# Up projection of a mixture-of-experts layer: the bias added over a whole PSUM bank by VectorE, the bounds applied by GpSimd

## The chip, the cores and the metric

The kernel runs on one core of a Trainium2 chip. The metric is device time in microseconds, the median of several executions. Its engines are TensorE (PE in the profile, PEld for its weight loads), VectorE (DVE), ScalarE (ACT), GpSimd (POOL) and SyncE (SP), which issues most DMAs. Each engine works through its own instructions in program order and waits on semaphores for the others.

## The reference, cut to what matters

The model is one layer on 1024 tokens of width 1024: a token mixer, then a channel mixer with 32 experts, of which every token uses four. The change lies in the channel mixer alone. For each expert and the token slots routed to it (`xb`):

```
up = xb @ w_up[e] + b_up[e]                     # 1024 -> 2048
x_glu, x_lin = split(up, 2)                     # gate half, linear half
x_glu = minimum(x_glu, 7)
x_lin = clip(x_lin, -7, 7)
act = x_glu * sigmoid(1.702 * x_glu) * (x_lin + 1)
y = act @ w_down[e] + b_down[e]                 # 1024 -> 1024
```

The rows `y` are weighted by the router's gates and added to the token's sum; a final norm ends the program. Everything is float32.

## The kernel before

**Where the time lies.** Up to about 590 us the kernel does the token mixer and the routing. The expert stage follows, and after it the last norm.

**Experts.** Expert r (in order of load) gets a fixed number of slots, `CAPS[r]`, from 210 down to 108. They run in the order `ORDER`, a small one and a large one in turn: 112, 210, 114, 192, 116, 182, 120, 174, 122, 168, 122, 164, 124, 160, 126, 158, 128, 154, 128, 150, 130, 148, 132, 146, 134, 142, 136, 140, 136, 138, 108, 108 slots. Twenty have more than 128. The last one (`tail`) is treated apart.

**Phases.** For an expert j the kernel has three phases: A computes the gate half of the up projection ("G"), B the linear half ("L"), D the down projection. Experts overlap: A(j), D(j-1), B(j), A(j+1), D(j), B(j+1) and so on. A phase has eight slots, one for each block k of 128 contracted rows; in slot k TensorE multiplies eight output blocks (m), each with three products of f16 parts (high by high, high by low, low by high; L1787 to L1789). The moving operand has as many columns as the expert has slots, n. The five experts above 170 slots or marked `tail` have phases of four output blocks instead.

**Weights.** SP loads one 128x1024 float32 piece for each slot into one of 14 staging buffers (`wf`, L1766). ScalarE makes its high f16 part (`wh`, L1886) and VectorE its low part (`wl`, L1887, which reads `wf` and `wh` from SBUF). The two are split six slots ahead of TensorE (`LOOK`), into seven buffers.

**PSUM.** A phase accumulates in a tile `ac` of three banks of 512 float32, two tiles taking turns. A bank holds `per = 512 // n` blocks: four up to 128 slots, three up to 170, two above.

**Epilogues.** The epilogue of a phase runs during the next phase: `run_phases` calls each of its pieces at a given slot, before that slot's matmuls, and after it the split for six slots on. Halves of four blocks (or two) are treated one after the other.

- Epilogue of A, during D: at slots 0 and 1 `clamp` writes `eg` from PSUM, one VectorE operation for each block, which adds the bias (one value per partition) and applies the upper bound (L1804). At slots 1 and 3 `gate` has ScalarE compute the sigmoid (`es`, L1809) and GpSimd multiply `eg` by it (L1810).
- Epilogue of B, during the next A: at slots 0 and 1 `lin` writes `el` in the same way (L1826); at slots 1 and 2 `prod` applies the lower bound and multiplies by `eg` (L1830); at slots 2 and 3 ScalarE writes the high part of the activation `aT` (`high`, L1837) and VectorE its low part (`low`, L1840). `aT` feeds the next D.
- Epilogue of D, during B: ScalarE moves the output to SBUF (`yT`, L1858) at slots 0 and 1; from slot 3 on TensorE turns it into rows (L1872), ScalarE scales them (`yr`, L1873), and GpSimd adds them to the sum in HBM by an indirect DMA (`acc_d`, L1875): at slot 4 for the first 128 rows, at slot 6 for the rest, where there is one.

**GpSimd's other work.** At slot 5 of each A it loads the slot list of a later expert (`ids`, L1720) and gathers the rows of the one after next (`xr`, L1730). All of this stands in GpSimd's one queue in program order. The rows are turned at the first slots of A (L1742, L1743).

Of the kernel before, what the change touches and what calls it, by code (L numbers as in the profile page):

```python
# [35 lines left out]
STRIDE = 1152  # L36
# [5 lines left out]
CAPS = [210, 192, 182, 174, 168, 164, 160, 158, 154, 150, 148, 146, 142, 140, 138, 136,  # L42
        136, 134, 132, 130, 128, 128, 126, 124, 122, 122, 120, 116, 114, 112, 108, 108]
# [80 lines left out]
def build(ctx, tc, A, out, dbg=None):  # L124
    nc = tc.nc
    V, S, G, PE, SY = nc.vector, nc.scalar, nc.gpsimd, nc.tensor, nc.sync
    dbg = dbg or {}
    MULT, ADD, SUB, MIN, MAX = OP.mult, OP.add, OP.subtract, OP.min, OP.max
# [6 lines left out]
    def pst(shape=(128, 512), dt=F32, tag="g"):  # L135
        return ps.tile(list(shape), dt, name=f"ps_{tag}", bufs=BANKS[tag])
# [117 lines left out]
    for r0, src in ((0, A["b_mod"]), (48, A["c"]), (56, A["norm1_w"]), (64, A["norm2_w"])):  # L254
        n = src.shape[1] // 128
# [62 lines left out]
    p = pst(tag="o")  # L318
# [77 lines left out]
    f = math.factorial  # L396
# [813 lines left out]
    for l in range(SL):  # L1210
        r = SL - 1 - l
# [16 lines left out]
    for i in range(-1, NT):  # L1228
        h = i + 1
        n = 2 if left["s5"] else 1  # L1230
# [317 lines left out]
    for i in range(NT):  # L1548
        h, b, t = i + 1, i - 1, i - 2
        hd, ob, ot, last = h < NT, 0 <= b, 0 <= t, i == NT - 1  # L1550
        f = lambda: fill(w3)
# [37 lines left out]
    t, b, i = NT - 3, NT - 2, NT - 1  # L1589
# [41 lines left out]
    SS = SW * SX  # L1631
    SA = 16.0
    with tc.manual_schedule():
# [6 lines left out]
        p = tpt()  # L1640
# [15 lines left out]
        p = tpt()  # L1656
# [14 lines left out]
        BALL = mc.tile([128, NE, 24], F32, name="BALL")  # L1671
# [26 lines left out]

    class Expert:
        def __init__(self, n, e, row, bias, q, tail=False):  # L1700
            self.n, self.get_e, self.get_row, self.bias, self.q = n, e, row, bias, q
            self.eid = None
            self.rows = [(0, min(n, 128))] + ([(128, n - 128)] if n > 128 else [])
            self.per = 512 // n
            every, lo, hi = list(range(8)), [0, 1, 2, 3], [4, 5, 6, 7]
            fits = 3 * self.per >= 8
            self.down = [every] if fits else [lo, hi]
            if fits and not tail:
                self.up = [[("G", every)], [("L", every)]]
            else:  # L1710
                self.up = [[("G", lo), ("L", lo)], [("G", hi), ("L", hi)]]
            self.xT = self.aT = self.yT = self.glu = self.final = None
# [39 lines left out]
    class Phase:  # L1752
# [41 lines left out]
        def halves(self):  # L1794
            return [(i, self.ms[i:i + self.nm // 2]) for i in range(0, self.nm, self.nm // 2)]

        def glu_pieces(self):
            x, n = self.x, self.x.n

            def clamp(i, ms):  # L1800
                if i == 0:
                    x.glu = mx.tile([128, self.nm, n], F32, name="eg", bufs=1)
                for q, m in enumerate(ms):
                    V.tensor_scalar(x.glu[:, i + q, :], self.loc(i + q), x.bias(m), 7.0 * SS, op0=ADD, op1=MIN)  # L1804

            def gate(i, ms):
                g = x.glu[:, i:i + len(ms)].rearrange("p m n -> p (m n)")
                s = mx.tile([128, len(ms) * n], F32, name="es", bufs=1)
                S.activation(s, g, AF.Sigmoid, scale=1.702 / SS)  # L1809
                G.tensor_tensor(g, g, s, op=MULT)  # L1810

            out = []
            for q, (i, ms) in enumerate(self.halves()):
                out += [(q, lambda i=i, ms=ms: clamp(i, ms)), (1 + 2 * q, lambda i=i, ms=ms: gate(i, ms))]
            return sorted(out, key=lambda t: t[0])

        def lin_pieces(self):
            x, n = self.x, self.x.n
            if x.aT is None:
                x.aT = mx.tile([128, 2, 8, n], F16, name="aT")  # L1820
            t = {}

            def lin(i, ms):
                t[i] = mx.tile([128, len(ms), n], F32, name="el")
                for q, m in enumerate(ms):
                    V.tensor_scalar(t[i][:, q, :], self.loc(i + q), x.bias(8 + m), 8.0 * SS, op0=ADD, op1=MIN)  # L1826
                t[i] = t[i].rearrange("p m n -> p (m n)")

            def prod(i, ms):
                V.scalar_tensor_tensor(t[i], t[i], -6.0 * SS, x.glu[:, i:i + len(ms)].rearrange("p m n -> p (m n)"),  # L1830
                                       op0=MAX, op1=MULT)

            def part(q, ms):
                return x.aT[:, q, ms[0]:ms[0] + len(ms), :].rearrange("p m n -> p (m n)")

            def high(i, ms):
                S.activation(part(0, ms), t[i], AF.Copy, scale=SA / (SS * SS))  # L1837

            def low(i, ms):
                V.scalar_tensor_tensor(part(1, ms), t[i], SA / (SS * SS), part(0, ms), op0=MULT, op1=SUB)  # L1840

            out = []
            for q, (i, ms) in enumerate(self.halves()):
                for at, f in ((0, lin), (1, prod), (2, high), (2, low)):
                    out.append((q + at, lambda i=i, ms=ms, f=f: f(i, ms)))
            return sorted(out, key=lambda t: t[0])

# [81 lines left out]
    def make(r):  # L1929
        def load(eng):  # L1930
            return eng.value_load(ordi[0:1, r:r + 1], min_val=0, max_val=NE - 1)

        return Expert(CAPS[r], lambda: load(SY), lambda q: load(q) * STRIDE, lambda m: BALL[:, r, m:m + 1], G,
                      r == ORDER[-1])

    class FinalNorm:
# [3 lines left out]
        def load(self, i):  # L1940
            x = self.x[i] = stg.tile([128, D], F32, name="wf")
            SY.dma_start(x, acc_d[i * 128:(i + 1) * 128, :])
# [91 lines left out]
    with tc.If(over > 0):  # L2034
        G.indirect_dma_start(out=acc_d[:, :], out_offset=bass.IndirectOffsetOnAxis(ap=ex[-1].ids[0][:, 0:1], axis=0),
                             in_=last.y, in_offset=None)
        bias_d = dram.tile([NE, 128, 24], F32, name="bias_d")
        for r in range(NE):
            SY.dma_start(bias_d[r], BALL[:, r, :])
        val = mc.tile([1, 4, 256], F32, name="oval")  # L2040
        v8 = [val[:, q, :].rearrange("p (r j) -> p r j", j=8) for q in range(4)]
        V.tensor_tensor_scan(val[:, 0, :], ones[0:1, 0:1].to_broadcast([1, 256]),
                             nbf.rearrange("p r j -> p (r j)"), 0.0, op0=MULT, op1=ADD)
        V.tensor_tensor(val[:, 0, :], val[:, 0, :], nbf.rearrange("p r j -> p (r j)"), op=MULT)
        V.tensor_copy(v8[1], ordf[:, 0:NE, None].to_broadcast([1, NE, 8]))
        V.scalar_tensor_tensor(v8[2], v8[1], float(STRIDE), cc("thr", 1).rearrange("p (r j) -> p r j", j=8),
                               op0=MULT, op1=ADD)
        V.tensor_copy(v8[3], cc("iota", 1)[:, 0:NE, None].to_broadcast([1, NE, 8]))
        vb = mc.tile([64, 4, 256], F32, name="ovb")
        for q in range(4):  # L2050
            p = tpt()
            PE.matmul(p[0:64, 0:256], ones[0:1, 0:64], val[:, q, :], start=True, stop=True)
            V.tensor_copy(vb[:, q, :], p[0:64, 0:256])
        V.tensor_scalar(vb[:, 0, :], vb[:, 0, :], -1.0, cc("pcol", 64), op0=ADD, op1=OP.is_equal)
        oc = mc.tile([64, 3], F32, name="ocol")
        ol = mc.tile([1, 3, 64], I32, name="olist")
        p = tpt()
        for q in range(3):
            V.tensor_tensor(vb[:, q + 1, :], vb[:, q + 1, :], vb[:, 0, :], op=MULT)
            V.tensor_reduce(oc[:, q:q + 1], vb[:, q + 1, :], op=ADD, axis=AX.X)  # L2060
            PE.transpose(p[0:1, q * 64:(q + 1) * 64], oc[:, q:q + 1], ident[0:64, 0:64])
        V.tensor_copy(ol.rearrange("p q s -> p (q s)"), p[0:1, 0:192])
        with tc.For_i(0, over, 1) as bi:
            e = SY.value_load(ol[0:1, 0, ds(bi, 1)], min_val=0, max_val=NE - 1)
            row = SY.value_load(ol[0:1, 1, ds(bi, 1)], min_val=0, max_val=(NE - 1) * STRIDE + T)
            ri = SY.value_load(ol[0:1, 2, ds(bi, 1)], min_val=0, max_val=NE - 1)
            bt = mx.tile([128, 24], F32, name="bt", bufs=1)
            SY.dma_start(bt, bias_d[ds(ri, 1)].rearrange("o p m -> (o p) m"))
            x = Expert(128, lambda: e, lambda q: row, lambda m: bt[:, m:m + 1], SY, True)
            x.load_ids()  # L2070
            x.gather()
            for _, t in x.turn_x():
                t()
            run_phases(x.phases("A") + x.phases("B") + x.phases("D"), {}, 3, 2)
            fin = FinalNorm()
            for i in range(NT):
                fin.load(i)
                fin.square(i)
                fin.store(i)
# [27 lines left out]
```

## Time and profile before

| | us |
|---|---|
| median of 3 executions | 1909.22 (1908.97 to 1916.93) |
| profiled execution, its own time | 1911.87 |
| span of its trace | 1910.2 |

| engine | busy us | share of the span |
|---|---|---|
| PE | 1753.9 | 92% |
| DVE | 1583.3 | 83% |
| ACT | 1236.3 | 65% |
| POOL | 575.1 | 30% |

The share of busy time is a mean over stages with different limits, so a stage is read by itself: its busy times, its waits, and the chain of work that ended last. A row of a timeline gives the start and the length of one instruction, or of several of one kind in a row (`x4`); in square brackets stands how long the engine stood idle before it, and what it then waited for. A wait is put down to whatever came last by the profile; where the engine named had long been done, it was another, often a DMA.

### The profile page before, as it was taken

The page shows a single profiled execution, that of the slowest core. Times are in us where ns is not written, and L with a number is a line of the kernel's source. Part 1 is how long each engine was busy: PE and PEld are TensorE (multiplying, and loading weights), DVE is VectorE, ACT ScalarE, POOL GpSimd, SP SyncE. Part 2 cuts the span into 40 slices and gives each one's busy share as a digit, 9 for nine tenths or more (in the row PEclk, how much of TensorE's full clock was granted, in tenths as well). Part 3 has the DMA queues.
Part 4 walks back from the last instruction along what each step waited for, and adds up shares of the span by engine and source line. Part 5 has one row for each costly group of instructions (what it writes and reads, how often), then busy time and mean ns, then how long its engine had stood idle before and what let it go on. Part 6 is the DMA issues. An engine that isn't in the chain of part 4 may idle for free.

```text
span 1910.2 us, 57330 instructions
## 1 busy us (share of the span) xinstructions
PE 1753.9 (92%) x23174; PEld 1559.7 (82%) x23174; DVE 1583.3 (83%) x2430; ACT 1236.3 (65%) x1714; POOL 575.1 (30%) x505
## 2 busy tenths in 40 slices
PE   6889988999974999999999989999999999999983
PEld 3756665556643899999999979999999999999973
DVE  7858677765576888888897969999999999999985
ACT  2722333212234777777787868888888888888874
POOL 3834110143434223132221413213133333233214
PEclk9989999999996999999999989999999999999997
DMA  8841246632229999999998989999999999999996
GB/s 293 285 103 39 59 148 201 215 128 71 72 81 287 335 317 288 355 327 336 329 346 285 365 268 380 368 367 372 361 371 355 366 365 341 369 374 354 364 327 206
DMA packets 189451, 533.54 MB, mean 279 GB/s; under 512 B 37710, under 2 KB 47880, under 8 KB 189148
## 3 DMA queue, kind: packets, MB, share of 16 engines
q1 hardware_dynamic: 167548, 490.92, 71.6%
q0 software_dynamic: 21344, 37.85, 8.3%
q8 instruction: 183, 3.00, 0.6%
q10 hardware_dynamic: 288, 1.05, 0.1%
q14 instruction: 88, 0.72, 0.1%
HBM read 489.81 MB, written 39.30 MB: 277 GB/s over the span
## 4 chain that ended last, share of the span: by engine, by line
PE 46%; DMA 12%; ACT 4%; DVE 3%; issue 3%; POOL 1%; SPq 0%; DVEq 0%; ACTq 0%; POOLq 0%
PE ac L1787 14%; PE ac L1788 14%; PE ac L1789 14%; DMA wf<-in_w_up_dram 10%; ACT wh L1886 3%; DVE wl L1887 2%; PE tp L1872 2%; PE tp L1742 2%; DMA wf<-in_w_down_dram 2%; DMA xr<-h2s,ids 1%; ACT yT L1858 1%; POOL fs L1948 0%; ACT yr L1873 0%; DMA idtab<-pairs,dest 0%; POOL fs L1949 0%
## 5 line engine op out<-in xcount | busy, mean ns | idle before, releaser
L1887 DVE SCALAR_TENSOR_TENSOR wl<-wf,wh 128x1024 f16<-128x1024 f32 x768 | 944.5, 1270 | 137.3 <-ACT wh L1886 127.5
L1886 ACT ACTIVATE wh<-wf 128x1024 f16<-128x1024 f32 x768 | 774.3, 1055 | 50.3 <-DMA wf<-in_w_up_dram 21.4
L1789 PE MATMUL ac<-xT,wl 128*128 128x122 f16 (+27 forms) x4096 | 770.3, 226 | 4.5 <-DVE wl L1887 4.5
L1787 PE MATMUL ac<-xT,wh 128*128 128x122 f16 (+27 forms) x4096 | 770.9, 226 | 3.2 <-DVE el L1826 1.4
L1788 PE MATMUL ac<-xT,wh 128*128 128x122 f16 (+27 forms) x4096 | 770.4, 226 | 0.6 <-ACT xT L1743 0.6
L1789 PEld LDWEIGHTS <-wl 128*128 128x128 f16 x6144 | 602.2, 98 | 10.9 <-DVE wl L1887 8.8
L1788 PEld LDWEIGHTS <-wh 128*128 128x128 f16 x6144 | 603.4, 98 | 5.5 <-issue 4.1
L1787 PEld LDWEIGHTS <-wh 128*128 128x128 f16 x6144 | 602.9, 98 | 5.5 <-ACT wh L1886 3.6
L1787 PE MATMUL ac<-aT,wh 128*128 128x122 f16 (+27 forms) x2048 | 380.0, 226 | 3.1 <-DVE eg L1804 2.0
L1789 PE MATMUL ac<-aT,wl 128*128 128x122 f16 (+27 forms) x2048 | 380.0, 225 | 1.8 <-DVE wl L1887 1.7
L1788 PE MATMUL ac<-aT,wh 128*128 128x122 f16 (+27 forms) x2048 | 380.0, 225 | 0.9 <-DVE aT L1840 0.9
L1875 POOL DMA_INDIRECT acc_d<-yr,ids x51 | 135.2, 2651 | 592.2 <-ACT yr L1873 409.0
L1810 POOL TENSOR_TENSOR eg<-eg,es 128x420 f32<-128x420 f32 (+28 forms) x74 | 102.5, 1385 | 301.7 <-ACT es L1809 301.7
L1858 ACT ACTIVATE yT<-ac,BALL,g2s 128x122 f32<-128x122 f32 (+27 forms) x256 | 97.7, 473 | 9.1 <-PE ac L1789 9.1
L1837 ACT ACTIVATE aT<-el 128x420 f16<-128x420 f32 (+28 forms) x74 | 45.2, 611 | 90.2 <-DVE el L1830 89.3
L1743 ACT COPY xT<-tp 128x1024 f16<-128x1024 f16 (+27 forms) x104 | 75.8, 730 | 29.9 <-PE tp L1742 29.5
L1730 POOL DMA_INDIRECT xr<-h2s,ids x52 | 85.7, 1647 | 30.8 <-issue 19.7
L1809 ACT ACTIVATE es<-eg 128x420 f32<-128x420 f32 (+28 forms) x74 | 44.8, 605 | 74.3 <-DVE eg L1804 72.2
L1742 PE MATMUL tp<-id,xr 128*128 128x128 f16 (+27 forms) x832 | 54.3, 204 | 29.6 <-DMA wf<-in_w_up_dram 22.8
L1872 PE MATMUL tp<-C,yT 128*128 128x128 f32 (+27 forms) x408 | 68.4, 281 | 13.4 <-ACT yT L1858 10.1
L1826 DVE TENSOR_SCALAR el<-ac,BALL 128x122 f32<-128x122 f32 (+27 forms) x256 | 75.9, 355 | 0.0
L1804 DVE TENSOR_SCALAR eg<-ac,BALL 128x122 f32<-128x122 f32 (+27 forms) x256 | 74.8, 355 | 0.0
(495 smaller groups left out, 2426.0 us busy)
## 6 DMA issues: line engine op xcount, KB each, us to landing
wf<-in_w_up_dram SPq DMA_DIRECT2D x512, 512.0 KB, 8.4
wf<-in_w_down_dram SPq DMA_DIRECT2D x256, 512.0 KB, 10.0
wst<-in_w_mod_dram SPq DMA_DIRECT2D x40, 512.0 KB, 4.4
wst<-in_w_in_dram SPq DMA_DIRECT2D x16, 576.0 KB, 5.5
x<-in_x_dram SPq DMA_DIRECT2D x16, 512.0 KB, 4.4
hTb<-hT_d SPq DMA_DIRECT2D x16, 512.0 KB, 5.4
wA<-in_w_mod_dram SPq DMA_DIRECT2D x8, 512.0 KB, 10.3
hT_d<-hTa SPq DMA_DIRECT2D x8, 512.0 KB, 5.5
```

The lines of the kernel that those rows point to most:

```text
L1730: G.indirect_dma_start(out=x, out_offset=None, in_=h2s[:, :], in_offset=bass.IndirectOffsetOnAxis(ap=self.ids[j][:, 0:1], axis=0))
L1742: PE.transpose(p[:, k, :], self.xr[j][:, kk_ * 128:(kk_ + 1) * 128], id16[0:c, 0:c])
L1787: PE.matmul(dst, h[:, ms], xh, start=k == 0 and m % x.per == 0, stop=False, skip_group_check=True)
L1788: PE.matmul(dst, h[:, ms], xl, start=False, stop=False, skip_group_check=True)
L1789: PE.matmul(dst, l[:, ms], xh, start=False, stop=k == 7, skip_group_check=True)
L1810: G.tensor_tensor(g, g, s, op=MULT)
L1826: V.tensor_scalar(t[i][:, q, :], self.loc(i + q), x.bias(8 + m), 8.0 * SS, op0=ADD, op1=MIN)
L1858: S.activation(x.yT[:, m, :], self.loc(i), AF.Identity, scale=g2s[:, m:m + 1], bias=x.bias(16 + m))
L1872: PE.transpose(p[0:c, m * 128:(m + 1) * 128], x.yT[:, q * 4 + m, r0:r0 + c], ident)
L1875: G.indirect_dma_start(out=acc_d[:, :], out_offset=bass.IndirectOffsetOnAxis(ap=x.ids[j][:, 0:1], axis=0), in_=y, in_offset=None, compute_ ...
L1886: S.activation(h, w, AF.Copy, scale=SW)
L1887: V.scalar_tensor_tensor(l, w, SW, h, op0=MULT, op1=SUB)
```

## The change

For all experts but the last, the bias and the bounds come apart. VectorE adds the biases of all blocks of a half that lie in one PSUM bank in a single TENSOR_TENSOR, with the bias broadcast over the slots. GpSimd then applies the bounds in place in SBUF, one TENSOR_SCALAR for each half: the upper bound for `eg`, both for `el`. `prod` on VectorE is left with a plain product. The sigmoid and the product of the gate come one slot later, and so do `prod`, `high` and `low`.

```diff
+        def add_bias(self, dst, i, count, b0):
+            x, n = self.x, self.x.n
+            a = i
+            while a < i + count:
+                k = min(i + count, (a // x.per + 1) * x.per) - a
+                o = (a % x.per) * n
+                V.tensor_tensor(dst[:, a - i:a - i + k, :],
+                                self.ac[:, a // x.per, o:o + k * n].rearrange("p (m n) -> p m n", m=k),
+                                x.bias(b0 + self.ms[a], k)[:, :, None].to_broadcast([128, k, n]), op=ADD)
+                a += k
...
             def clamp(i, ms):
                 if i == 0:
                     x.glu = mx.tile([128, self.nm, n], F32, name="eg", bufs=1)
+                if not x.tail:
+                    g = x.glu[:, i:i + len(ms)]
+                    self.add_bias(g, i, len(ms), 0)
+                    g = g.rearrange("p m n -> p (m n)")
+                    G.tensor_scalar(g, g, 7.0 * SS, None, op0=MIN)
+                    return
                 for q, m in enumerate(ms):
                     V.tensor_scalar(x.glu[:, i + q, :], self.loc(i + q), x.bias(m), 7.0 * SS, op0=ADD, op1=MIN)
...
-            out = []
+            out, late = [], int(not x.tail)
             for q, (i, ms) in enumerate(self.halves()):
-                out += [(q, lambda i=i, ms=ms: clamp(i, ms)), (1 + 2 * q, lambda i=i, ms=ms: gate(i, ms))]
+                out += [(q, lambda i=i, ms=ms: clamp(i, ms)), (1 + 2 * q + late, lambda i=i, ms=ms: gate(i, ms))]
...
             def lin(i, ms):
                 t[i] = mx.tile([128, len(ms), n], F32, name="el")
-                for q, m in enumerate(ms):
-                    V.tensor_scalar(t[i][:, q, :], self.loc(i + q), x.bias(8 + m), 8.0 * SS, op0=ADD, op1=MIN)
+                if x.tail:
+                    for q, m in enumerate(ms):
+                        V.tensor_scalar(t[i][:, q, :], self.loc(i + q), x.bias(8 + m), 8.0 * SS, op0=ADD, op1=MIN)
+                else:
+                    self.add_bias(t[i], i, len(ms), 8)
                 t[i] = t[i].rearrange("p m n -> p (m n)")
+                if not x.tail:
+                    G.tensor_scalar(t[i], t[i], 8.0 * SS, -6.0 * SS, op0=MIN, op1=MAX)

             def prod(i, ms):
-                V.scalar_tensor_tensor(t[i], t[i], -6.0 * SS, x.glu[:, i:i + len(ms)].rearrange("p m n -> p (m n)"),
-                                       op0=MAX, op1=MULT)
+                g = x.glu[:, i:i + len(ms)].rearrange("p m n -> p (m n)")
+                if x.tail:
+                    V.scalar_tensor_tensor(t[i], t[i], -6.0 * SS, g, op0=MAX, op1=MULT)
+                else:
+                    V.tensor_tensor(t[i], t[i], g, op=MULT)
...
+            late = int(not x.tail)
             for q, (i, ms) in enumerate(self.halves()):
-                for at, f in ((0, lin), (1, prod), (2, high), (2, low)):
+                for at, f in ((0, lin), (1 + late, prod), (2 + late, high), (2 + late, low)):
                     out.append((q + at, lambda i=i, ms=ms, f=f: f(i, ms)))
```

The rest of the diff hands `tail` to the expert and lets `bias` return several blocks' values.

## Rows read from the trace of the kernel before

**Rows 1.** The page, part 4: the chain that ended last, its shares by engine.

```profile
PE 46%; DMA 12%; ACT 4%; DVE 3%; issue 3%; POOL 1%; SPq 0%; DVEq 0%; ACTq 0%; POOLq 0%
```

**Rows 2.** The same chain in order of time, its longest pieces: start us, us, what.

```profile
1097.81 30.94 DMA wf<-in_w_up_dram
...
1141.24 0.61 PE tp L1872 x4
...
1803.09 0.67 DVE aT L1840
```

**Rows 3.** Busy us by stretch: PE, PEld, DVE, ACT, POOL; then clock, DMA share, GB/s.

```profile
700.00:1141.00 441.00, 425.36 (x6353) 416.25 (x6350) 373.21 (x462) 340.95 (x451) 108.86 (x72) 0.98 0.95 322
1141.00:1803.00 662.00, 661.76 (x10777) 655.98 (x10778) 628.09 (x768) 566.83 (x749) 205.25 (x124) 1.00 1.01 365
...
1682.58:1758.56 75.98, 75.98 (x1253) 75.09 (x1251) 72.21 (x89) 65.66 (x89) 24.58 (x13) 1.00 1.00 360
```

**Rows 4.** All waits of PE from 1141 to 1803 us: total us, times, longest.

```profile
PE tp L1872 <- ACT yr L1873: 0.8, 1, 0.8
```

**Rows 5.** Groups by line, 1141 to 1803 us, columns as in the page's part 5.

```profile
L1875 POOL DMA_INDIRECT acc_d<-yr,ids x32 | 91.8, 2868 | 343.6 <-ACT yr L1873 215.9 <-ACT wh L1886 82.2 <-ACT xT L1743 36.0
...
L1804 DVE TENSOR_SCALAR eg<-ac,BALL 128x136 f32<-128x136 f32 (+14 forms) x136 | 39.8, 354 | 0.0
```

**Rows 6.** DVE in order of time: start us, us, line, operation, count.

```profile
1234.89 3.50 DVE L1887 SCALAR_TENSOR_TENSOR wl<-wf,wh 128x1024 f16<-128x1024 f32 x3
...
1240.60 1.24 DVE L1804 TENSOR_SCALAR eg<-ac,BALL 128x158 f32<-128x158 f32 x4
1241.76 5.01 DVE L1887 SCALAR_TENSOR_TENSOR wl<-wf,wh 128x1024 f16<-128x1024 f32 x3
```

**Rows 7.** POOL in the same stretch: start us, us, line, operation.

```profile
1240.45 1.62 POOL L1810 TENSOR_TENSOR eg<-eg,es 128x632 f32<-128x632 f32 x1 [2.44 <-ACT es L1809]
1242.96 1.59 POOL L1810 TENSOR_TENSOR eg<-eg,es 128x632 f32<-128x632 f32 x1 [0.89 <-ACT es L1809]
```

**Rows 8.** Two DVE groups by form, whole span.

```profile
L1426 DVE TENSOR_TENSOR x<-ps_s,g1s 128x512 f32<-128x512 f32 x14 | 9.6, 683 | 0.0
...
L1826 DVE TENSOR_SCALAR el<-ac,BALL 128x136 f32<-128x136 f32 x16 | 4.6, 350 | 0.0
```

**Rows 9.** Two POOL groups, whole span.

```profile
L877 POOL MEMSET kbd<- 128x512 f32 x2 | 1.0, 524 | 0.0
...
L1347 POOL TENSOR_SCALAR Sr<-Sr 64x96 f32<-64x96 f32 x28 | 12.5, 447 | 45.4 <-DVE Sr L1346 43.5
```

**Rows 10.** DVE at one linear epilogue.

```profile
1682.58 1.15 DVE L1826 TENSOR_SCALAR el<-ac,BALL 128x136 f32<-128x136 f32 x4
...
1685.08 0.72 DVE L1830 SCALAR_TENSOR_TENSOR el<-el,eg 128x544 f32<-128x544 f32 x1
```

**Rows 11.** POOL around the same epilogue.

```profile
1676.59 1.92 POOL L1875 DMA_INDIRECT acc_d<-yr,ids  x1 [11.96 <-ACT yr L1873]
1687.99 4.28 POOL L1875 DMA_INDIRECT acc_d<-yr,ids  x1 [9.48 <-ACT wh L1886]
1691.81 1.12 POOL L1720 DMA_DIRECT2D ids<-idtab  x1
```

**Rows 12.** PE there: first instructions of the gate phase and of the down phase.

```profile
1681.28 0.61 PE L1742 MATMUL tp<-id,xr 128*128 128x128 f16 x8
...
1694.64 0.22 PE L1787 MATMUL ac<-aT,wh 128*128 128x136 f16 x1
```

**Rows 13.** POOL at another second scatter.

```profile
1571.71 1.37 POOL L1875 DMA_INDIRECT acc_d<-yr,ids  x1 [8.58 <-ACT wh L1886]
1572.70 1.62 POOL L1720 DMA_DIRECT2D ids<-idtab  x2
```

**Rows 14.** DVE at that time.

```profile
1571.27 1.20 DVE L1826 TENSOR_SCALAR el<-ac,BALL 128x146 f32<-128x146 f32 x4
```

**Rows 15.** Waits of SP's DMA queue, 700 to 1141 us.

```profile
SPq L1766 <- DVE wl L1887: 125.4, 115, 3.5
```

More of the change, by code (lines that the diff above doesn't have):

```diff
@@ L1700, in __init__ @@
         def __init__(self, n, e, row, bias, q, tail=False):
-            self.n, self.get_e, self.get_row, self.bias, self.q = n, e, row, bias, q
+            self.n, self.get_e, self.get_row, self.bias, self.q, self.tail = n, e, row, bias, q, tail
             self.eid = None
@@ L1931, in load @@
             return eng.value_load(ordi[0:1, r:r + 1], min_val=0, max_val=NE - 1)
-        return Expert(CAPS[r], lambda: load(SY), lambda q: load(q) * STRIDE, lambda m: BALL[:, r, m:m + 1], G,
+        return Expert(CAPS[r], lambda: load(SY), lambda q: load(q) * STRIDE, lambda m, k=1: BALL[:, r, m:m + k], G,
                       r == ORDER[-1])
@@ L2068, in build @@
             SY.dma_start(bt, bias_d[ds(ri, 1)].rearrange("o p m -> (o p) m"))
-            x = Expert(128, lambda: e, lambda q: row, lambda m: bt[:, m:m + 1], SY, True)
+            x = Expert(128, lambda: e, lambda q: row, lambda m, k=1: bt[:, m:m + k], SY, True)
             x.load_ids()
```

## The prediction

> **What bounds the kernel now.** I read the chain that ended last first: TensorE holds 46% of it, the DMA 12%, VectorE 3% [rows 1]. Its longest DMA piece ends at 1128.75, and of its long pieces none begins between 1141.24 and 1803.09 [rows 2], so I cut the expert stage there and took busy times by stretch [rows 3]. From 700 to 1141 TensorE is busy for 425 of 441 us and the weights arrive late now and then. From 1141 to 1803 TensorE is busy for 661.8 of 662 us at granted clock 1.00 and waits for others for 0.8 us in total [rows 3, 4]. VectorE is at 628 of 662 us there: not the bound, but 5% from it. The change works in this place, so the question is what it does to VectorE's 5%, and to the order in which VectorE and GpSimd wait for each other.
>
> One pair of experts in that stretch takes 75.98 us with VectorE busy for 72.21 [rows 3]. Per expert: 38.0 us of TensorE against 36.1 of VectorE. All sums below are per expert of about 136 slots; 17 experts have their G epilogue in the stretch (136 instructions of 8 each) [rows 5].
>
> **Bias additions (VectorE, removed and added).** The four-fold groups of 128x158 and 128x136 last 1.24 us [rows 6] and 1.15 us [rows 10]: 0.09 us for 88 columns, 1.02 ns a column. One 128x136 alone is 0.350 us [rows 8], so three more take 0.80: 0.27 us each back to back, of which 0.14 are columns and 0.13 belong to the instruction. A 128x512 TENSOR_TENSOR from PSUM takes 0.683 us [rows 8]: the same column rate. So a wider addition saves 0.13 us for each instruction that goes. With 129 to 170 slots a bank holds three blocks, so a half of four blocks is cut 3+1 or 2+2: 16 instructions become 8, and 8 x 0.13 = **1.0 us** is saved per expert. With up to 128 slots 16 become 4, 1.6 us. The broadcast bias could make it slower than the row; bounds 0 to 1.6, I take 1.0. The product in `prod` stays one pass over the same columns: nothing.
>
> **Clamps (GpSimd, added).** Four per expert, each over about 544 columns in SBUF. No such row exists. From below: a 128x512 MEMSET, 0.52 us, which reads nothing [rows 9]; from above: the two-input product, 1.6 us for 632 columns [rows 7], so 1.4 for 544. The only real TENSOR_SCALAR is 64x96 at 0.447 us [rows 9]; with 448 more columns at 0.8 to 2 ns it lies at 0.8 to 1.3. I take **0.9 us**.
>
> GpSimd has time for that (205 of 662 us busy [rows 3]); VectorE pays. Three `wl` back to back take 3.50 us; three beside the second GpSimd product take 5.01, and the product lasts 1.59 [rows 6, 7]. VectorE thus loses 1.51 us, the whole product. The first product lies beside four PSUM-reading TENSOR_SCALARs, which keep their 1.24 us. The Trainium skill, page "SBUF — State Buffer", section "Who interferes with whom", says that a VectorE instruction with two SBUF inputs and a GpSimd instruction that reads SBUF exclude each other for a whole instruction, and one with a single SBUF input doesn't; these rows agree, 1.51 lost of 1.59 against none. It speaks against the change: the additions (one SBUF input) were never in the way, the clamps are.
>
> So of the four clamps, G's first lies beside the second addition and L's first in a wait of VectorE (below): free. The other two meet `wl` or `prod`: 2 x 0.9 = **+1.8 us**. And the gate moves one slot later: its first product, hidden today beside the second group, now meets `wl`: **+1.4 us**.
>
> VectorE per expert: 36.1 - 1.0 + 1.8 + 1.4 = **38.3 us against 38.0 of TensorE.** The relief is turned into a small excess.
>
> **The new wait.** Program order on GpSimd puts L's clamps behind the accumulating scatters of the expert before. The second scatter (every expert over 128 slots) waits until the first has landed: of the 32 scatters in the stretch 18 are first ones, which wait for their rows (215.9 us), and 14 second ones, 9 us each (82.2 + 36.0 + the 9.5 left of 343.6 us; the profile names ACT lines long done for most) [rows 5]. Today nothing urgent is queued behind it. In the quoted event the first scatter starts at 1676.59, the second at 1687.99, and GpSimd is free for the next instruction at 1691.81 [rows 11]. The linear epilogue starts at 1682.58 and the product already at 1685.08 [rows 10]. With the change, VectorE would add (0.8), split, add, split, and be at the moved `prod` at about 1687.0, where it must stand until the clamp behind the scatter is done. All its splits are queued behind `prod`, ScalarE's `high` waits for it, and TensorE's next phase, beginning at 1694.64 [rows 12], needs them.
>
> When is the clamp done? The second scatter holds GpSimd for 3.8 us beside dense splits [rows 11], but for 1.0 (until the next instruction) where VectorE did PSUM work [rows 13, 14]. The clamp then starts between 1689.0 and 1691.8 and ends between 1689.9 and 1692.7: 8.6 to 11.4 us after TensorE entered the phase (1681.28). At the first event the six prepared slices cover most of this. But with 38.3 us of work in 38.0 VectorE doesn't win the lead back, so the steady state counts. From the product's start until the first slice of the phase after next is split, VectorE has nine splits (1.15 each back to back, 10.4), two products and two low parts (0.65 each, 2.6), the gate half's two pairs of bias additions (1.6), two clamps' worth of standing (1.8) and one product's (1.4): 17.8 us. That makes 26.4 to 29.2 us after the phase began; TensorE wants that slice after 13.4 (1681.28 to 1694.64 [rows 12]) plus the down phase's 192 matmuls at 0.0606 us (1253 in 75.98 [rows 3]), 11.6, together 25.0 us. It stands **1.4 to 4.2 us** per event. In that steady state VectorE comes to `prod` about when the scatter is issued and idles for part of it, so I go below the middle: **2.4 us**.
>
> **The rest.** Three experts without such an event: 0.3 each. Of 20 second scatters, 6 lie outside the stretch, where TensorE already waits for weights (15.6 us idle in 441 [rows 3]): 0 to 3 us each, I take 0.5. PSUM is released by the additions, a little earlier than today; the down projection doesn't need it sooner: nothing, as TensorE waits for no bank [rows 4]. `load_ids` and the gathers stand two clamps (1.8 us) later in GpSimd's queue; their rows are used a whole expert (38 us) on, which hides that; without this cover it would be 1.8 each. The SP queue gets nothing new. The last expert keeps its old code.
>
> Sum: 14 x 2.4 + 3 x 0.3 + 6 x 0.5 = 37.5 us on the profiled execution's 1911.87, so 1949.4; that execution lies 2.65 us over the median of 1909.22, so **1947 us**.
>
> **Rivals.**
> (A) *The cover holds.* Clamps near the MEMSET price, 0.5 us: VectorE has 36.1 - 1.0 + 1.4 + 1.0 = 37.5 us of work, and the event comes to 8.2 + 17.0 - 25.0 = 0.2 us, or to nothing if the moved product hides as today. TensorE stays the bound: 1909 us, at most 1915. The Trainium skill ("GPSIMD Engine Reference", section "4.1 Engine selection") calls one-input operations on GpSimd roughly line rate; no run here shows it, and by it this case would hold. Against: the product beside `wl` was never hidden, and GpSimd stands behind the scatter whatever the clamp costs. Chance 0.22.
> (B) *Faster.* Place: 700 to 1141, where the SP queue waits 125.4 us for `wl` to free a staging buffer [rows 15]. If VectorE's relief frees buffers sooner, DMA starts sooner; eleven experts at 1.0 to 1.6 us give at most 14 us, so 1895 us. It decides if a clamp costs VectorE under about 0.3 us and the scatter does not hold it. For it: the DMA pieces in the chain. Against: TensorE's whole idle time there is 15.6 us, so nearly all of it would have to go. Chance 0.12.
> (C) *Much slower.* Clamps cost what the two-input product costs, 1.4 us: 36.1 - 1.0 + 1.4 + 2.8 = 39.3 us of work, and the event, with the scatter at 1.0 to 3.8 us, 9.1 to 11.9 + 18.8 - 25.0 = 2.9 to 5.7, say 4.5: 14 x 4.5 + 3 x 1.3 + 6 = 73 us, 1982 us. For it: the 64x96 row is dear for its size. Chance 0.15.
> The forecast has 0.51.
>
> **How the numbers follow.** Its own range is 1.4 to 4.2 us for 14 events and 0 to 3 for six: 1930 to 1987, the upper end with the long scatter throughout. The range for 8 in 10 takes in (A) and the nearer part of (C), not (B): 1908 to 1985. A measurement of this kernel tells about 0.5% (9.5 us) from no change. Slower: the forecast and (C), 0.66; within: (A), 0.22; faster: (B), 0.12.
>
> **What would show it.** In the changed profile, between 1141 and the tail: TENSOR_TENSOR additions of about 0.7 us in place of four TENSOR_SCALARs; GpSimd TENSOR_SCALARs near 0.9 us; VectorE waiting for GpSimd's `el` before the product, some 1 to 3 us after each expert over 128 slots; `wl` means above 1.27 us; and TensorE waiting for `wl` or `aT`, which it never does now. I am wrong if TensorE stays full with the lag on VectorE, or if VectorE's busy share falls there: then the clamps do not collide as the products do.

## The result and the profile after

The changed kernel takes 2018.18 us (2010.01 to 2022.95) beside 1910.31 us of the kernel before on the same chip: a ratio of 1.0552 [1.0528, 1.0576], some 108 us. The forecast was 1947 us with a range up to 1985. The direction was right, the size was missed by a factor of nearly three. The profiled execution has a span of 2020.8 us.

The page of the changed kernel, part 4, the chain that ended last (against [rows 1], where TensorE held 46%):

```profile
DMA 3%; issue 2%; DVE 2%; POOL 1%; ACT 1%; PE 1%; DVEq 0%; POOLq 0%; ACTq 0%
```

and its first piece in order of time:

```profile
1805.11 1.96 DMA acc_d<-yr,ids
```

These shares sum to 10% of the span, against 69% before: followed back from the end, the chain breaks off at 1805 us. It says nothing of the stretch from 1141 to 1803, which has to be read from busy times and waits. Busy times by stretch, columns as in [rows 3]; the third line is one expert's cycle:

```profile
700.00:1141.00 441.00, 417.93 (x6208) 407.09 (x6206) 360.37 (x357) 331.14 (x437) 165.49 (x123) 0.99 0.95 317
1141.00:1803.00 662.00, 618.60 (x9527) 587.18 (x9524) 546.55 (x539) 497.45 (x666) 255.82 (x175) 0.99 0.93 323
1593.44:1636.83 43.39, 40.39 (x623) 37.99 (x621) 35.56 (x37) 32.44 (x45) 16.84 (x12) 1.00 0.94 321
```

From 1141 to 1803 us TensorE's weight loads fell from 655.98 to 587.18 us, a loss of 69 us; PE's own column shows only 43 of them, since the ends of matmuls are modelled, so PEld is the column to read here. The Trainium skill, page "Perfetto Trace Analysis", section "Identifying the Most-Contended Engine", advises the same, and the matmul counts agree (9527 for 10777, 12% fewer, where 69 of 662 us are 10%). VectorE and ScalarE are less busy than before, too. The granted clock is 0.99 beside 1.00. So nothing is saturated: the engines wait for each other in a ring. A cycle of 43.4 us stands against 38.0 in [rows 3].

Where TensorE stands: PEld groups of the changed kernel in that stretch, idle time behind the second bar.

```profile
L1789 PEld LDWEIGHTS <-wl 128*128 128x128 f16 x2959 | 289.1, 98 | 36.3 <-DVE wl L1914 34.0 <-issue 2.0
L1899 PEld LDWEIGHTS tp<-C,yT 128*128 128x128 f32 (+13 forms) x216 | 23.5, 122 | 32.7 <-ACT yT L1885 21.8 <-ACT yr L1900 9.1
```

and the same two of the kernel before:

```profile
L1789 PEld LDWEIGHTS <-wl 128*128 128x128 f16 x3344 | 325.8, 97 | 0.0
L1872 PEld LDWEIGHTS tp<-C,yT 128*128 128x128 f32 (+15 forms) x248 | 23.6, 118 | 2.0 <-ACT yr L1873 1.0
```

36 us are lost waiting for VectorE's splits, 33 waiting for ScalarE's output of the down phase. The second place is in no step of the prediction. Who stands in front of them, waits from 1141 to 1803 us of the changed kernel (total us, times, longest):

```profile
DVE wl L1914 <- ACT wh L1913: 67.2, 92, 3.2
ACT es L1827 <- POOL eg L1819: 52.5, 16, 3.6
...
DVE el L1857 <- POOL el L1850: 44.7, 11, 4.7
...
ACT es L1827 <- POOL eg L1828: 25.1, 16, 1.7
```

The third line is the forecast wait: `prod` for the linear bounds, 4.1 us each. The second and fourth are new waits of ScalarE: 3.3 us an expert at the first sigmoid for GpSimd's bound, 1.6 us at the second for GpSimd's product, because `es` is one buffer (`bufs=1`) that this product gives back. The first line is what follows: VectorE's splits wait for `wh`, 67.2 us against 27.9 before.

GpSimd's groups in the stretch, against [rows 5]:

```profile
L1819 POOL TENSOR_SCALAR eg<-eg 128x512 f32<-128x512 f32 (+14 forms) x32 | 66.7, 2084 | 95.6 <-DVE eg L1804 94.3
L1828 POOL TENSOR_TENSOR eg<-eg,es 128x512 f32<-128x512 f32 (+14 forms) x32 | 60.4, 1886 | 13.8 <-ACT es L1827 12.5
...
L1850 POOL TENSOR_SCALAR el<-el 128x512 f32<-128x512 f32 (+13 forms) x30 | 32.5, 1084 | 19.2 <-DVE el L1804 17.6
```

The gate's bound, one operation, takes 2.08 us; the linear bounds, two in one instruction over as many columns, 1.08. Part of the difference is the company: the gate's bounds run beside splits, and of the linear pair below the first runs while VectorE stands (0.62 us), the second beside `prod` (1.15). The other part is the operation itself: in experiment 6 a gate's bound took 1.50 us with VectorE standing (last section).

One expert of 132 slots and the gate half after it, in three timelines of the changed kernel. GpSimd (against [rows 11]):

```profile
1598.74 1.43 POOL L1902 DMA_INDIRECT acc_d<-yr,ids  x1 [9.29 <-DMA acc_d<-yr,ids]
1600.24 0.62 POOL L1850 TENSOR_SCALAR el<-el 128x528 f32<-128x528 f32 x1
1600.94 1.15 POOL L1850 TENSOR_SCALAR el<-el 128x528 f32<-128x528 f32 x1
...
1611.63 2.49 POOL L1819 TENSOR_SCALAR eg<-eg 128x584 f32<-128x584 f32 x1 [5.29 <-DVE eg L1804]
1614.20 1.78 POOL L1819 TENSOR_SCALAR eg<-eg 128x584 f32<-128x584 f32 x1
1616.06 2.27 POOL L1828 TENSOR_TENSOR eg<-eg,es 128x584 f32<-128x584 f32 x1
1619.13 1.57 POOL L1828 TENSOR_TENSOR eg<-eg,es 128x584 f32<-128x584 f32 x1 [0.80 <-ACT es L1827]
```

VectorE (against [rows 10]) and ScalarE:

```profile
1593.44 0.77 DVE L1804 TENSOR_TENSOR el<-ac,BALL 128x396 f32<-128x396 f32 x2
...
1600.90 0.71 DVE L1857 TENSOR_TENSOR el<-el,eg 128x528 f32<-128x528 f32 x1 [3.74 <-POOL el L1850]
...
1615.83 3.59 DVE L1914 SCALAR_TENSOR_TENSOR wl<-wf,wh 128x1024 f16<-128x1024 f32 x2 [1.36 <-ACT wh L1913]
```

```profile
1614.16 0.69 ACT L1827 ACTIVATE es<-eg 128x584 f32<-128x584 f32 x1 [3.38 <-POOL eg L1819]
...
1618.36 0.69 ACT L1827 ACTIVATE es<-eg 128x584 f32<-128x584 f32 x1 [1.63 <-POOL eg L1828]
```

and TensorE's weight loads in the linear phase that follows:

```profile
1617.10 0.10 PEld L1789 LDWEIGHTS <-wl 128*128 128x128 f16 x1 [1.15 <-DVE wl L1914]
1619.47 0.10 PEld L1789 LDWEIGHTS <-wl 128*128 128x128 f16 x1 [0.85 <-DVE wl L1914]
1621.83 0.10 PEld L1789 LDWEIGHTS <-wl 128*128 128x128 f16 x1 [0.86 <-DVE wl L1914]
...
1629.11 0.31 PEld L1899 LDWEIGHTS tp<-C,yT 128*4 128x4 f32 x4 [0.81 <-ACT yr L1900]
```

Read down, that is the ring. VectorE stands 3.7 us behind the scatter and then works without a break until 1614.46; GpSimd's bounds for the gate take 2.49 us beside its splits and 1.78 where it mostly stands; ScalarE stands 3.4 us for the first of them and 1.6 for the buffer; its high parts come late; VectorE waits for those, and TensorE for the low parts, slice after slice. The linear phase takes 18.7 us (1615.85 to 1634.55), a linear phase of the kernel before 13.4 (1706.00 to 1719.43, 140 slots against 146).

### The profile page after: what moved, and what is told of

It is laid out like the page before. It is cut to its first block, busy times and chain, and to the rows that moved or that the text cites. A ratio compares the mean times of both kernels' runs of the same rounds, so it can differ in the third digit from the quotient of the medians.

```text
span 2020.8 us, 57084 instructions
## 1 busy us (share of the span) xinstructions
PE 1797.8 (89%) x23174; PEld 1569.7 (78%) x23174; DVE 1567.6 (78%) x2138; ACT 1229.5 (61%) x1714; POOL 733.4 (36%) x645
## 5 line engine op out<-in xcount | busy, mean ns | idle before, releaser
L1914 DVE SCALAR_TENSOR_TENSOR wl<-wf,wh 128x1024 f16<-128x1024 f32 x768 | 973.9, 1300 | 176.7 <-ACT wh L1913 170.2
L1902 POOL DMA_INDIRECT acc_d<-yr,ids x51 | 93.7, 1837 | 541.5 <-ACT yr L1900 355.0
L1819 POOL TENSOR_SCALAR eg<-eg 128x420 f32<-128x420 f32 (+27 forms) x70 | 127.5, 1821 | 200.8 <-DVE eg L1804 198.0
L1828 POOL TENSOR_TENSOR eg<-eg,es 128x420 f32<-128x420 f32 (+28 forms) x74 | 120.9, 1633 | 40.7 <-ACT es L1827 38.0
L1899 PE MATMUL tp<-C,yT 128*128 128x128 f32 (+27 forms) x408 | 86.3, 298 | 33.0 <-ACT yT L1885 18.3
L1857 DVE TENSOR_TENSOR el<-el,eg 128x420 f32<-128x420 f32 (+27 forms) x70 | 52.0, 743 | 80.8 <-POOL el L1850 80.8
L1899 PEld LDWEIGHTS tp<-C,yT 128*128 128x128 f32 (+27 forms) x408 | 44.9, 126 | 58.6 <-ACT yT L1885 41.4
L1850 POOL TENSOR_SCALAR el<-el 128x420 f32<-128x420 f32 (+27 forms) x70 | 70.0, 1000 | 48.0 <-DVE el L1804 44.6
```

The costliest lines, as they stand in the source:

```text
L1819: G.tensor_scalar(g, g, 7.0 * SS, None, op0=MIN)
L1850: G.tensor_scalar(t[i], t[i], 8.0 * SS, -6.0 * SS, op0=MIN, op1=MAX)
L1899: PE.transpose(p[0:c, m * 128:(m + 1) * 128], x.yT[:, q * 4 + m, r0:r0 + c], ident)
L1914: V.scalar_tensor_tensor(l, w, SW, h, op0=MULT, op1=SUB)
```

## The experiments

Theory S is that new waits at GpSimd, of VectorE at `prod` and of ScalarE at the sigmoid, use up the lead of six prepared slices. Rival P says that GpSimd's and VectorE's accesses to SBUF hold each other up wherever they stand, and rival H that the linear bounds behind the second scatter are all of it. All ratios are to the kernel before on the same chip, with a 95% interval.

**1. The gate half alone.** `lin` and `prod` as before the change, the rest of the change kept.

```diff
-                    self.add_bias(t[i], i, len(ms), 8)
...
-                    G.tensor_scalar(t[i], t[i], 8.0 * SS, -6.0 * SS, op0=MIN, op1=MAX)
+                for q, m in enumerate(ms):
+                    V.tensor_scalar(t[i][:, q, :], self.loc(i + q), x.bias(8 + m), 8.0 * SS, op0=ADD, op1=MIN)
```

> Only the gate half gets the wide additions and GpSimd's bound; the linear half is as before. Theory S (two stands that together use up the six prepared slices: VectorE at the product behind the second scatter, then ScalarE at the sigmoids behind clamps that wait for VectorE's splits): one stand alone is mostly covered, 1912 to 1945 us. Rival P (the port: every clamp costs VectorE its own time, wherever it stands, some 108 us over 140 clamps): about half of the loss, 1960 to 1975 us. Rival H (the scatter at the head of GpSimd's queue alone): no loss, 1905 to 1915 us.

1948.04 us, 1.0186 [1.0158, 1.0214]: 3 us above theory S's span, below rival P's and far above rival H's. Its two groups of weight loads in the stretch:

```profile
L1789 PEld LDWEIGHTS <-wl 128*128 128x128 f16 x3171 | 309.4, 98 | 0.8 <-DVE wl L1906 0.4
L1891 PEld LDWEIGHTS tp<-C,yT 128*128 128x128 f32 (+15 forms) x240 | 24.8, 118 | 29.9 <-ACT yT L1877 16.3 <-ACT yr L1892 11.9
```

TensorE hardly waits for a split here (0.4 us in all), but 29.9 us for ScalarE's output. The gate half has its own cost, and it goes through ScalarE: rival H alone is out.

**2. The linear half alone.** The mirror image: `clamp` and the gate's slots as before the change.

> Only the linear half gets the wide additions, GpSimd's bounds and the later product; the gate half is as before. S: the stand of about 4 us at the product is partly covered when the gate half takes nothing, 1920 to 1965 us. P: about half of the loss, 1955 to 1970 us. H: nearly all of it, 1990 to 2018 us.

1961.37 us, 1.0258 [1.0229, 1.0286]: inside the spans of theory S and of rival P, so it doesn't decide between them, and below rival H's.

```profile
L1789 PEld LDWEIGHTS <-wl 128*128 128x128 f16 x3158 | 308.8, 98 | 20.7 <-DVE wl L1908 19.6 <-issue 0.6
L1893 PEld LDWEIGHTS tp<-C,yT 128*128 128x128 f32 (+15 forms) x240 | 23.1, 121 | 8.2 <-ACT yr L1894 3.9 <-ACT yT L1879 3.3
```

Here it is the splits. The halves alone cost 2.6% and 1.9%, together 4.4%; the whole costs 5.5%, so some 1.1% (21 us) comes of their meeting.

**3. The second scatter later.** The whole change; the scatter of the rows from 129 on is issued at slot 3 of the next phase, behind the linear bounds in GpSimd's queue.

```diff
-                if q == 1:
+                def scatter():
                     G.indirect_dma_start(out=acc_d[:, :],
...
+                if q == 1 and j == 0:
+                    scatter()
+                elif q == 1:
+                    deferred.append((3, scatter))
```

> The whole change, but the second scatter of an expert is issued four slots into the next phase, behind the linear half's clamps. S: the stand at the product goes (VectorE waits for GpSimd's el under 15 us in total instead of 81), the sigmoids' stand is left and is covered in part, 1930 to 1970 us. P: unchanged, 2005 to 2020 us. H: 1905 to 1915 us.

1940.33 us, 1.0145 [1.0116, 1.0175], inside theory S's span: VectorE's wait for the linear bounds is gone from the list, and with it some three quarters of the loss. The two sigmoid waits stay (53.4 and 26.8 us in the stretch), and so does most of what experiment 1 cost. Yet the linear bounds now take 1.56 us each in place of 1.08, as VectorE no longer stands beside them: a longer operation for which nobody waits cost nothing.

**4. The bounds on VectorE.** `V.tensor_scalar` in place of `G.tensor_scalar`, all else of the change kept.

> The whole change, but VectorE itself applies the bounds in SBUF; no clamp on GpSimd. S: no wait on GpSimd is left; VectorE gets about 36.1 - 1.0 + four passes over 544 columns of SBUF at 0.4 to 0.7 us, so 37 to 38 of 38.0 us per expert, 1905 to 1930 us. P: 1905 to 1930 us as well. H: 1905 to 1930 us. It says what the wide additions are worth once the bounds cost something on VectorE, and rules out that they themselves are slow.

1910.47 us, 0.9991 [0.9974, 1.0007]. Taken together, the wide additions, the moved slots and the extra pass over SBUF cost nothing (against experiment 7 the pass alone costs 0.5%); the whole loss belongs to the bounds' being on GpSimd. VectorE is busy for 634.0 of 662 us, more than the changed kernel's 546.6, and TensorE is full (661.2). The same bounds inside VectorE's own queue are cheap here, the handover to GpSimd isn't.

**5. The sigmoids later as well.** Experiment 3 with the gate at slots 3 and 5 (`1 + 2 * q + 2 * late`).

> The run with the late second scatter, and the gate's sigmoids and products moved from slots 2 and 4 to slots 3 and 5. S (the 27 us left there are ScalarE standing at the sigmoids for clamps that get their turn late, so that high parts and then slices come late): ScalarE's wait for GpSimd's eg falls from 135 us in total to under 50, the time to 1912 to 1925 us. P (the 27 us are clamps and products excluding VectorE, wherever they stand): 1935 to 1942 us, as without the move.

1931.58 us, 1.0091 [1.0074, 1.0108]: between the two, and outside both spans. Over the whole run the wait for the bound fell from 86.1 us in experiment 3 to 61.5, the one for the product stayed (49.2 and 52.4). That makes 114 us where theory S had under 50: one slot is not enough.

**6. Bounds that nobody waits for.** The kernel before, with 140 extra operations on GpSimd of the same kind and size, which write a scratch buffer.

```diff
+                    G.tensor_scalar(scr[:, 0:len(ms) * n], g, 7.0 * SS, None, op0=MIN)
...
+                    G.tensor_scalar(s, s, 8.0 * SS, -6.0 * SS, op0=MIN, op1=MAX)
```

> The kernel before, with the change's 140 clamps issued on GpSimd on top: the gate half's read eg and write a scratch tile, the linear half's work on the scratch tile alone; no other engine waits for any of them. Only the collision in SBUF is left. S: 1908 to 1922 us, with clamps of 0.7 to 2 us in the trace and wl a little longer. P: VectorE loses 0.7 to 1 us for each of 140 clamps, 1960 to 2010 us.

1980.85 us, 1.0346 [1.0325, 1.0366]. Theory S as it stood fails: it had this free, and rival P's number came. The trace has another reason. GpSimd and ScalarE at one gate epilogue:

```profile
1460.26 2.33 POOL L1808 TENSOR_SCALAR bf<-eg 128x520 f32<-128x520 f32 x1 [12.46 <-DVE eg L1805]
1462.68 2.99 POOL L1814 TENSOR_TENSOR eg<-eg,es 128x520 f32<-128x520 f32 x1
```

```profile
1465.70 0.64 ACT L1813 ACTIVATE es<-eg 128x520 f32<-128x520 f32 x1 [2.99 <-POOL eg L1814]
```

Nobody waits for the bound, but GpSimd's product stands behind it, and ScalarE's second sigmoid waits for that product, since it needs the buffer back. Over the whole run (total us, times, longest):

```profile
ACT es L1813 <- POOL eg L1814: 81.9, 31, 3.6
```

The theory was revised: what costs is ScalarE standing at a sigmoid, for the bound or for the one buffer. Experiment 9 puts that against rival P.

**7. No bounds at all.** The whole change with both bounds left out: this kernel computes something else wherever a bound would act.

> The whole change without its clamps: no upper or lower bound is applied for any expert but the last (that part of the computation is left out); wide additions and later slots stay. Both theories: 1903 to 1915 us, TensorE full as before, VectorE with some 1 us less per expert. If it were slower, the later slots or the wide additions would carry part of the loss.

1902.73 us, 0.9938 [0.9921, 0.9954]. That is all that the wide additions, with the later slots, can bring (theory S and rival P had 1903 us and more). Compared by the starts of the down phases, its gain is complete by 1026 us (7.7 us); from 1108 to 1804 us it stays between 6.1 and 6.6. There VectorE has 610.7 us of work in 662 and TensorE 662.0.

**8. The linear half with the scatter later.** Experiments 2 and 3 together.

> Only the linear half of the change, with the second scatter issued four slots into the next phase. S: the whole loss of the linear half (51 us) was the place behind the scatter, so 1903 to 1918 us and no wait of VectorE for GpSimd's el beyond 10 us in total. P: the linear clamps still cost their time, 1950 to 1965 us.

1910.13 us, 0.9977 [0.9962, 0.9992]. The linear half costs nothing once its bounds don't stand behind the scatter. Of 2.6% nothing is left, so that cost was the place in the queue.

**9. Experiment 6 with two sigmoid buffers.** The second sigmoid writes a buffer of its own; every bound is still there.

```diff
-                s = mx.tile([128, len(ms) * n], F32, name="es", bufs=1)
+                s = mx.tile([128, len(ms) * n], F32, name="es", bufs=1) if i == 0 else es2[:, 0:len(ms) * n]
```

> The kernel before with the same 140 bounds on GpSimd that nobody waits for (1980.85 us), and one more thing changed: the two sigmoids of an expert write two buffers instead of one. Theory S, revised: a bound on GpSimd costs only by what makes ScalarE stand at a sigmoid; here that was the one sigmoid buffer, which GpSimd's first product gives back after it has stood behind the bound (31 waits, 81.9 us in all, longest 3.6). With two buffers those waits go and the time is 1909 to 1925 us. Rival P (GpSimd's bounds and VectorE's two-input splits hold each other up wherever they stand, and that is the cost): the bounds are all still there, so 1955 to 1985 us.

1925.66 us, 1.0071 [1.0046, 1.0096], against 1.0346 with one buffer: four fifths of the cost were the buffer (the time lies 0.7 us over the revised theory's span). Rival P would have kept it all. In the stretch TensorE's weight loads are back at 650.0 us, though GpSimd is busier there (402 us) than in any other run:

```profile
L1815 POOL TENSOR_TENSOR eg<-eg,es 128x512 f32<-128x512 f32 (+14 forms) x34 | 121.8, 3583 | 2.8
```

GpSimd's product takes 3.58 us where it took 1.46 before, and no engine's waits for it are in the list. About half of the loss that is left, 7 us by the starts of the down phases, is there by 1071 us; its cause was not pursued.

**10. The whole change with two sigmoid buffers.** The second buffer of experiment 9 is the only edit.

> The whole change (2018 us), only with two sigmoid buffers. Theory S, revised: the waits of a sigmoid for GpSimd's product (34, 50.7 us in all, 1.5 us each and some 3 us an expert) go; those for the bound itself (93.2 us) and VectorE's for the linear bounds behind the second scatter (80.8 us) stay. 1965 to 1995 us. Rival (the bounds' own durations and the scatter are the cost, the buffer is not): 2005 to 2025 us.

1986.91 us, 1.0392 [1.0363, 1.0420]: 1.6% (31 us) less than the change. TensorE's wait for ScalarE's output fell from 32.7 to 11.7 us in the stretch, the one for the splits nearly stayed (36.3 and 33.3).

**11. All three mends.** Experiment 5 with two sigmoid buffers.

> The whole change with the second scatter and both sigmoids later (1931.6 us), and two sigmoid buffers. Theory S, revised: the 52.4 us of waits for the product go, the 61.5 us for the bound stay; of the 21 us left over the kernel before, half or more goes: 1910 to 1922 us. Rival P: nothing of it goes, since GpSimd's and VectorE's work are the same: 1927 to 1936 us.

1914.41 us, 1.0009 [0.9994, 1.0025]. The loss is gone with all of GpSimd's bounds still in place. Busy times from 1141 to 1803 us, columns as in [rows 3], and the two largest waits of ScalarE that are left:

```profile
1141.00:1803.00 662.00, 662.00 (x10765) 655.93 (x10764) 630.55 (x612) 569.28 (x748) 319.04 (x193) 1.00 1.00 366
```

```profile
ACT aT L1865 <- DVE el L1859: 32.9, 32, 1.5
ACT es L1829 <- POOL eg L1821: 32.0, 25, 2.3
```

The sigmoid still waits 1.3 us for the bound, 25 times, and TensorE is full: a wait that the lead covers costs nothing.

**12. The bounds out of everyone's way.** Gate: wide additions, the sigmoid taken from the unbounded sum (beyond the bound it differs from the reference's by less than 7e-6). Linear half: bounds and then the product with the sigmoid on GpSimd; VectorE's product applies the gate's bound, `V.scalar_tensor_tensor(t, g, 7.0 * SS, t, op0=MIN, op1=MULT)`. The scatter later, two sigmoid buffers, `prod` one slot later.

> A version in which no sigmoid waits for a bound. Gate half: the biases in wide additions, the sigmoid taken straight from them (its input unbounded: above the bound the sigmoid is 1 to about 7e-6). Linear half: wide additions, bounds on GpSimd, then GpSimd multiplies by the sigmoid; VectorE's product applies the gate's bound in its own operation. Second scatter late, two sigmoid buffers, the product one slot later. GpSimd does the bounds of one half and the products of one half, VectorE no bounds in PSUM. Theory S: what the kernel without any bounds took, 1900 to 1908 us. Rival P (four GpSimd operations with VectorE's splits beside them cost what they did): 1915 us and more.

1924.04 us, 1.0071 [1.0049, 1.0093]: theory S missed by 16 us, and the time lies where rival P had it. Yet not one sigmoid waits for GpSimd, and by the starts of the down phases it loses nothing from 1071 to 1770 us (+10.1 and +9.7 us), with the same four operations and splits in every expert, which speaks against P's reason. Most of the loss lies before that, where weights arrive late: from 590 to 1141 us TensorE waits for `yT` for 14.4 us against 7.6 before, in six waits each. Why ScalarE is later there was not pursued. No version that applies the bounds beats the kernel before by 0.5%; the nearest is experiment 8 with 0.2%.

## Why the prediction was wrong, step by step

- **"TensorE is the bound from 1141, VectorE 5% from it."** Right, and it holds further than I used it: in experiment 7 VectorE has 17 us less to do there, and nothing is gained.
- **Bias additions, 1.0 us saved.** The saving was rather larger: the two additions of a half take 0.77 us in the timeline above (132 slots), where four operations took 1.15 [rows 10]; four halves make 1.4 to 1.5 us. It is worth nothing in this stretch.
- **A bound at 0.9 us on GpSimd.** One price for two operations, and wrong for both. With VectorE standing a linear bound takes 0.62 us for 528 columns (timeline above) and a gate's bound 1.50 for 520 (last section), outside the 0.8 to 1.3 on either side. On average over the stretch they took 1.08 and 2.08.
- **Collisions: "VectorE thus loses 1.51 us, the whole product", so 1.8 + 1.4 us more for VectorE.** Wrong in who pays. The mean split rose from 1.271 to 1.302 us: 24 splits an expert x 0.03 = 0.7 us, not 3.2. GpSimd's own operations grew longer: the product took 1.89 us (1.46 before), and the gate's bound 2.08, where it takes 1.57 for 544 columns with VectorE standing (experiment 6). The Trainium skill, page "SBUF — State Buffer", section "Who interferes with whom", says that issue order decides which of the two blocks. The runs agree that it can be either (last section). The prediction took one row in which VectorE lost [rows 6, 7] for the rule.
- **"G's first lies beside the second addition ...: free."** This is the step that failed. I priced the bounds by what they take from VectorE and never asked who waits for them: ScalarE, in program order, with `wh`, `yT` and `yr` queued behind the sigmoid. For an expert without a second scatter the prediction had 0.3 us in all; experiment 1, in which no bound stands behind a scatter, measured 1.86%, some 35 us or 1.1 us for each of 31 experts, and its trace has it at `yT` and `yr`. The single `es` buffer, which is in the code, appears in no step; experiments 9 to 11 show what it is worth.
- **The new wait behind the scatter.** Mechanism, place and the first late slice were right: the first bound was done about 10.1 us after the phase began (forecast 8.6 to 11.4), and the slice that 26.4 to 29.2 us were given for came after 26.35 us. Experiment 8 confirms the cause. The price in the stretch was right as well: by the starts of the down phases, experiment 2 loses 27.4 us between 1108 and 1804 us of the kernel before, 2.0 for each of 14 events (forecast 2.4). Mis-sized was the term for the six events outside, 6 x 0.5 and at most 6 x 3: 18.5 us are lost by 1108 and 8 after 1804, over 4 us each. Why an event costs more there was not pursued.
- **The rivals.** (A), cover holds, is what happens when the waits are mended (experiments 8 and 11), not with the change as made. (B) needs earlier staging buffers; without any bounds the gain was 11.8 us by the ratio, near its bound of 14, and SP's wait for `wl` from 700 to 1141 us fell from 125.4 [rows 15] to 45.0, but the bounds ate it. (C) came nearest in time, 1982 us, for a reason that was not at work: its 1.4 us a bound comes near the gate's, but its sum hung on the linear bounds behind the scatter, and there `prod` waited for one of 0.62.

What the sum lacked besides is that two waits on one ring cost more together than apart: 1.9% and 2.6% alone, 5.5% together. Between 1108 and 1804 us, counted as above, the gate half alone loses 30.1 us, the linear half alone 27.4, the whole change 74.0. And the late scatter takes off 4.1 points with the gate half in place, where the linear half's own cost is 2.6.

## What to carry to other kernels

Before moving an operation to another engine, list who waits for its result and what is queued behind the waiter on that engine; the operation's length mattered here only beyond the slack of that waiter. Take its price from a row of the very form: two bounds of one size differed by a factor of 2.4 with VectorE standing. A single buffer that a slow engine hands back is a wait as real as a data dependence, and doubling it (or moving an instruction one or two slots) is worth trying before giving the idea up. And where one engine is full and another has 5% to spare, relief of the other bought nothing there: without any bounds at all the merged additions brought 0.6%, none of it in the stretch that TensorE fills.

## What the runs showed of the hardware

A run of VectorE splits can shut GpSimd out for its whole length. Experiment 9, GpSimd and VectorE:

```profile
1444.46 8.68 POOL L1815 TENSOR_TENSOR eg<-eg,es 128x520 f32<-128x520 f32 x1
...
1455.67 1.31 POOL L1815 TENSOR_TENSOR eg<-eg,es 128x520 f32<-128x520 f32 x1
```

```profile
1443.96 8.03 DVE L1895 SCALAR_TENSOR_TENSOR wl<-wf,wh 128x1024 f16<-128x1024 f32 x7
1452.93 1.30 DVE L1895 SCALAR_TENSOR_TENSOR wl<-wf,wh 128x1024 f16<-128x1024 f32 x1 [0.94 <-ACT wh L1894]
```

The first product takes 8.68 us; it starts while VectorE is in its run of seven splits, which take 1.15 us each as they do alone, and ends 1.15 us after the last of them (1451.99). The second, of the same size, takes 1.31 us; it starts 0.1 us after a bound of GpSimd's, and now the seven splits beside it take 9.34 us, 1.31 more than the seven before:

```profile
1454.61 9.34 DVE L1895 SCALAR_TENSOR_TENSOR wl<-wf,wh 128x1024 f16<-128x1024 f32 x7 [0.38 <-ACT wh L1894]
```

So either engine can lose: in these two cases the one that came into the other's unbroken run waited, and GpSimd for seven instructions of VectorE's. The Trainium skill, page "SBUF — State Buffer", section "Who interferes with whom", speaks of the whole of one instruction. In experiment 6 the same product took 2.99 us and again ended 1.14 us after VectorE's last split (1464.53): there ScalarE stood, so the splits ran dry and GpSimd got in. ScalarE's stand for GpSimd is thus also what ended GpSimd's.

The form of GpSimd's operation counted as much as its company. Experiment 6 again, the second bound of the gate (one operation, MIN) and VectorE around it:

```profile
1465.76 1.50 POOL L1808 TENSOR_SCALAR bf<-eg 128x520 f32<-128x520 f32 x1
```

```profile
1462.18 2.35 DVE L1894 SCALAR_TENSOR_TENSOR wl<-wf,wh 128x1024 f16<-128x1024 f32 x2
1467.32 3.46 DVE L1894 SCALAR_TENSOR_TENSOR wl<-wf,wh 128x1024 f16<-128x1024 f32 x2 [2.79 <-ACT wh L1893]
```

VectorE does nothing from 1464.53 to 1467.32, and the bound still takes 1.50 us (nine such cases in the stretch, 504 to 560 columns: 1.47 to 1.61). The linear bounds, MIN and MAX in one instruction, take 0.59 to 0.67 us for 496 to 592 columns in the eleven cases of the changed kernel in which VectorE stands. That the second operation makes the difference is not shown, since the instructions differ in more than that; in the changed kernel, where both work in place, the gate's second bound above takes 1.78 us for 584 columns with splits beside it for 0.4 us of them. No run gave the gate's bound a second, idle operation, so how much of ScalarE's wait is the price of this form, and could be had back by another, stays open.
